# Spacing and offsets of the weight places in a hybrid encoder layer: 1,056 columns apart instead of 1,024, one small offset for four kinds of products

## The chip, the core and the metric

The kernel runs on one core of a Trainium2 chip. The metric is the device time of one execution in microseconds (us); of several runs the median is given. The engines are named as in the profile: PE (TensorE, matrix products, with PEld for its weight loads), DVE (VectorE), ACT (ScalarE), POOL (GpSimd), SP (SyncE, which here only issues transfers).

## What is computed

One layer of an encoder on 512 tokens of width 1,024, all in float32:

```python
h = modulate(rmsnorm(x, norm_ffn1), sh1, sc1)
x = x + 0.5 * g1 * swiglu(h, w_ffn1_in, w_ffn1_out)         # 1024 -> 2 x 2816 -> 1024
h = modulate(rmsnorm(x, norm_mix), sh2, sc2)
qa, ka, va, qb, kb, vb, ga, gb = split(h @ w_in)
ya = window_gqa_sink(rope(qa), rope(ka), va) @ w_branch_a   # 8 heads on 2, window 128
yb = rmsnorm(diff_attention(rope(qb), rope(kb), vb)) @ w_branch_b   # 4 heads, dense
x = x + g2 * ((sigmoid(ga) * ya + sigmoid(gb) * yb) @ w_out)
h = modulate(rmsnorm(x, norm_ffn2), sh3, sc3)
x = x + 0.5 * g3 * swiglu(h, w_ffn2_in, w_ffn2_out)
```

The nine vectors sh, sc and g come from `silu(c) @ w_mod + b_mod`.

## The kernel before

**Three products for one.** Every float32 operand is split into a high part (rounded to the type float32r) and a low part (the rest, float32r too). A product of two such operands is three products on the PE: high times high, high times low, low times high (`mm3` at L173 to L176, `two` at L443 to L445, the opening loop at L681, the projections at L1125 to L1127 and L1144 to L1146). What stays in the array is 128 x 128; what is streamed past it, the moving operand, is 256 or 512 columns wide. A 256-wide product is made wherever a token half is worked on by itself, and in the units described next; all others are 512 wide.

**Stages.** Feed-forward 1: an opening with eight outputs (L681), two plain outputs pairs (L174 to L176), then units of a seven-product scheme on 2 x 2 blocks (class `Unit`, products `a11`, `s1`, `a12`, `a22`, `s4`, `s2`, `s3`, each of 24 matmuls 256 wide), between them the output projection in four chunks (class `Out1`; its last chunk is called `final`, and the last four of its eight rows, `LAST_1`, are made by token halves). Then the mixer: gates, projections `project` and `project_pairs` (here the weights are the moving operand and the hidden state the stationary one), the two attentions interleaved, the two branch projections (`branch`, 512 wide for `w_yb`, by halves for `w_ya`), and the mixing product `w_mix` (eight rows, the last two, `LAST`, by halves). Then feed-forward 2: one plain pair of outputs (class `Plain`), the unit `lead` and then units of the same scheme to the end.

**The places of weights.** A weight tile of 128 x 1,024 columns is loaded into a buffer `raw` (or `u`), and ACT and DVE write its high and low part (`split_from`, L190) into a place. The places lie in two long tiles, `high` and `low`, five places in each (`HILO`), taken in turn by `high_low`; a place that a unit still holds is passed over. Place i begins at column i x 1,024 plus an offset that the caller names, `aside`:

```python
ASIDE = 16
FAR = 64
STEP, STEP_1 = 8, 56
BRANCH_ASIDES = (STEP, ASIDE, ASIDE, ASIDE), (ASIDE, ASIDE, 0, 0)
MIX_ASIDES = 0, 0, 0, 0, 0, 0, ASIDE, ASIDE
```

The units use 16 columns, the opening, the projections, the gates (but one) and the 512-wide rows of `w_mix` use none, `Out1` uses 64 for its 512-wide rows (its tiles have at most 768 columns) and 56 or 16 for its last four rows, and `project_pairs` 16. A full tile of 1,024 columns that is set aside by 16 reaches 16 columns into the next place. A column is 4 bytes.

**The order of the work.** The PE's order is written out by hand (`run_items`, `boundary`, and the list of timed pieces in `Line`); loads are asked for a fixed number of items ahead (`ASK`, `MAKE`). Writing a place waits for the last matmul that read the columns it overlaps.

**Memory.** A core has 229,376 bytes in each partition. Tiles are laid out in the order of their first use, each rounded up to 32 bytes; tiles of one tag share its buffers. The hidden states and the other split operands are in `b8` (8,192 bytes each) and `u4` (4,096 bytes). The last byte used is 229,120.

Of the kernel before, what the change touches and what calls it, by code (L numbers as in the profile page):

```python
# [18 lines left out]
P = 128  # L19
# [79 lines left out]

ASIDE = 16  # L100

FAR = 64


STEP, STEP_1 = 8, 56
BRANCH_ASIDES = (STEP, ASIDE, ASIDE, ASIDE), (ASIDE, ASIDE, 0, 0)
MIX_ASIDES = 0, 0, 0, 0, 0, 0, ASIDE, ASIDE

# [26 lines left out]
def layer(ctx: ExitStack, tc: tile.TileContext, a: dict):  # L135
# [61 lines left out]
    def high_low(n=1024, aside=0, holder=None):  # L197
        while turn[0] % HILO in holders:
            turn[0] += 1
        i = turn[0] % HILO  # L200
        turn[0] += 1
        if holder:
            holders[i] = holder
        i = i * 1024 + aside
        return tuple(t[:, i : i + n] for t in parts)
# [20 lines left out]
    S.activation(small(8), half, AF.Silu)  # L226
    ones = keep([P, P], "ones")
    V.memset(ones, 1.0)
    ident = keep([P, P], "ident")
    make_identity(nc, ident)  # L230

    par = keep([P, NPAR], "par")
    x = [xt() for _ in range(NC)]
    parts, modv = [], []
    for nm, n in (("high", 6), ("low", 9)):
        parts.append(keep([P, HILO * 1024 + ASIDE], nm, F32R))
        modv += [keep([P, NC], f"mod{v}") for v in range(len(modv), n)]
    sub8, lam_s, nlam = (keep([P, n], nm) for nm, n in (("sub8", 1), ("lam_s", 2), ("nlam", 1)))

# [44 lines left out]
    class Norm:  # L284
# [41 lines left out]
        def sums(self, sq, r, first, last):  # L326
            if first:
                self.st[r.start] = bank("op" if r.start else "tp")
            for t in range(r.start // P, r.stop // P):
                i = 2 * (t - r.start // P)  # L330
                PE.matmul(
                    self.st[r.start][:, i : i + 2], sq[:, t * P : (t + 1) * P], ones[:, 0:2],
                    start=first and i == 0, stop=last and (t + 1) * P == r.stop, skip_group_check=True,
                )
# [112 lines left out]
    class Unit:  # L447
# [14 lines left out]

        in_order = ()
        spare, roomy, apart, more = ("s1",), (), (), {"s1": ("s2", "a11"), "s2": ("s4", "a12"), "a11": ("s3", "a21")}
# [16 lines left out]
        def prepare(self, q):  # L481

            if q in self.ready:
                return
            self.ask(q)
            n = self.depth * 2 * P
            if q in self.apart:
                both = b8().rearrange("p a b -> p (a b)")
                hi, lo = both[:, 0:n], both[:, 1024 : 1024 + n]
            else:  # L490
                hi, lo = high_low(n, ASIDE, (self, q))
            t = self.at[q]
# [110 lines left out]
    hh, hl = new_h()  # L603
    ccol = keep([P, 3 * NC], "ccol")[:, 0:NC]
    nc.scalar.dma_start(ccol, a["c"])
# [4 lines left out]
    with tc.manual_schedule(engines=BOUND | {mybir.EngineType.SP, mybir.EngineType.Pool}):  # L610
# [16 lines left out]
        warm(3)  # L627
        w1, pos = {}, []

        def first_loads(k):  # L630
            scale = mod_load(SC1, k)
            if k == 0:
                pos.append(keep([P, NT], "pos", I32))
# [140 lines left out]
    row = u4(F32).rearrange("p a b -> p (a b)")[:, 0:NROW]  # L774
    pos = pos[0]
    freq = keep([P, HD // 2], "freq")
# [56 lines left out]
    class Out1:  # L833
# [13 lines left out]

        def by_halves(self, m):
            return self.final and m >= NC - LAST_1

        def prepare(self, m):
            if m not in self.ready:
                self.ask(m)
                aside = FAR if not self.by_halves(m) else STEP_1 if m == NC - LAST_1 else ASIDE
                if self.final and m == 0:
                    while turn[0] % HILO != 1:
                        turn[0] += 1
                t = self.ready[m] = high_low(self.depth * P, aside, (self, m))
                with tc.issue_after(copied[0]):
                    split_from(*t, self.at[m])  # L860
# [52 lines left out]
    with tc.manual_schedule(engines={mybir.EngineType.SP, mybir.EngineType.Pool}):  # L913
# [4 lines left out]
        for q in range(4, 2 * PLAIN):  # L918

            w, sums_from = loaded1, split[1]  # L920
            if q < 5:
                with tc.issue_after(split[0]), tc.issue_after(split[1]):
                    loaded1 = [load_split(a["w1i"][1, k], aside=ASIDE) for k in range(2)]
            behind = split[1]
# [60 lines left out]
    NF = HD // 2  # L985
    posf = keep([P, NT], "posf")
    V.tensor_copy(posf, pos)
# [70 lines left out]

    def load_main(src, aside=0):

        raw = sbuf("raw", [P, 1024], F32, RAW)
        nc.sync.dma_start(raw, src)
        hi, lo = high_low(aside=aside)
# [67 lines left out]
    def project_pairs(srcs, then):  # L1131
# [3 lines left out]
        for u, src in enumerate(srcs):  # L1135
            wh, wl = load_main(src, ASIDE)
            for t in range(NT):
# [22 lines left out]
    def gates(more=lambda: True):  # L1160
        while gate_next[0] < 16 and more():
            j = gate_next[0]
            gate_next[0] += 1

            wh, wl = load_main(a["w_gate"][j], ASIDE * (j == EARLY_A))
            out = bank("acc")
            for k in range(NC):
                o = k * P
                mm3(out, wh[:, o : o + P], wl[:, o : o + P], hh[k], hl[k], k == 0, k == NC - 1)
                yield MM3  # L1170
            gate_end(j, out)
# [73 lines left out]
    rqb = keep([P, NT, 8], "rqb")  # L1245
    nrqb = keep([P, NT, 8], "nrqb")
    ob_h, ob_l = b8(), b8()
# [145 lines left out]
    def tables_a():  # L1393
# [3 lines left out]
        ka = sbuf("ka", [P, 2, T], F32R, 1)  # L1397
        wa.update(k=(ka[:, 0, :], ka[:, 1, :]), rq=keep([P, NT, 8], "rqa"))

# [197 lines left out]

    def branch(w, j0, o_h, o_l, then, load, r=FULL[0], asides=(0, 0, 0, 0)):
        for u in range(4):
            with tc.issue_after(banded_last[0]):  # L1600
                wh, wl = load(w[u], aside=asides[u])
            for i in range(2):
# [10 lines left out]
    def main():  # L1613
# [31 lines left out]
        for i, r in enumerate(HALVES):  # L1645
            line.drain(lambda: done["a"] >= 2 * i + 2)
            yield from branch(a["w_ya"], 0, *wa["o"], then_b, load_split, r, BRANCH_ASIDES[i])

# [13 lines left out]
    for m in range(NC):  # L1662
        w = load_split(a["w_mix"][m], aside=MIX_ASIDES[m])

# [369 lines left out]
```

## Time and profile before

| | |
|---|---|
| three runs | 1045.71, 1048.36, 1048.68 us; median 1048.36 |
| the profiled execution | 1044.11 us, of which the span from first to last instruction is 1042.3 us |
| granted PE clock in it | 0.999 |
| busy: PE, DVE, ACT, POOL | 99%, 75%, 55%, 16% of the span |
| matmuls | 7,348, and as many weight loads |
| moved by DMA | 220.92 MB |

In the profile a matmul's end is modelled and consecutive matmuls overlap, so its duration (276 ns for most 256-wide ones) is not what it costs. What it costs is the distance from its start to the start of the next one, which is read from the starts in the timeline. The timeline's times begin at the start of the span.

### The profile page before, as it was taken

Reading aid. Unit: us, or ns where it says so; the run is one execution under the profiler, and the core shown is the slowest. Engines: PE = TensorE matmul, PEld = TensorE weight load, DVE = VectorE, ACT = ScalarE, POOL = GpSimd, SP = SyncE. Lnnn points to the kernel's source line nnn. Section 1 sums busy time; section 2 is a strip of 40 time slices with the busy share of each in tenths; the row PEclk is TensorE's granted clock in tenths of the full one; section 3 lists DMA queues with packets and bytes.
Section 4 is the critical chain, followed back from the end, with each engine's and each line's share of the span. In section 5 each row is a group of like instructions: output and inputs, shape, how many; then the busy total and the mean of one; then the engine's idle time right before and its main releaser. Section 6 shows DMA issues by size and latency. Waiting matters only on the chain.

```text
span 1042.3 us, 18751 instructions
## 1 busy us (share of the span) xinstructions
PE 1034.8 (99%) x7348; PEld 953.2 (91%) x7348; DVE 785.5 (75%) x1436; ACT 575.6 (55%) x948; POOL 165.7 (16%) x190
## 2 busy tenths in 40 slices
PE   9999999999999999999999999999999999999998
PEld 6889899899998998899888888989999999999998
DVE  6886667567796679859772588976899777877867
ACT  6664335234454442667785855525867556655553
POOL 1101110110110100543333101001111111112110
PEclk9999999999999999999999999999999999999999
DMA  9977786966984459796646834974498998989874
GB/s 366 346 218 187 242 235 198 275 173 180 259 207 150 149 203 410 232 261 140 179 97 184 242 124 158 366 229 112 98 238 190 244 226 206 231 216 220 208 150 127
DMA packets 68793, 220.92 MB, mean 212 GB/s; under 512 B 8288, under 2 KB 10976, under 8 KB 68704
## 3 DMA queue, kind: packets, MB, share of 16 engines
q1 hardware_dynamic: 46224, 146.52, 38.7%
q0 software_dynamic: 19344, 68.70, 35.1%
q10 hardware_dynamic: 3136, 4.51, 1.2%
q8 instruction: 57, 0.93, 0.3%
q14 instruction: 32, 0.26, 0.1%
HBM read 209.46 MB, written 10.23 MB: 211 GB/s over the span
## 4 chain that ended last, share of the span: by engine, by line
PE 93%; DVE 3%; ACT 3%; issue 0%; DMA 0%; POOL 0%; DVEq 0%; ACTq 0%; POOLq 0%
PE acc L443 7%; PE acc L444 7%; PE acc L445 7%; PE sc L443 6%; PE sc L445 6%; PE sc L444 6%; PE sc L174 5%; PE sc L175 5%; PE sc L176 5%; PE acc L174 4%; PE acc L176 4%; PE acc L175 4%; PE acc L1125 2%; PE acc L1126 2%; PE acc L1127 2%; PE tp L1203 1%
## 5 line engine op out<-in xcount | busy, mean ns | idle before, releaser
L190 ACT CAST high<-raw 128x1024 fp32r<-128x1024 f32 (+2 forms) x160 | 155.9, 985 | 149.8 <-PE sc L175 37.7
L190 DVE TENSOR_TENSOR low<-raw,high 128x1024 fp32r<-128x1024 f32 (+2 forms) x160 | 181.3, 1141 | 49.4 <-ACT high L190 48.5
L443 PE MATMUL acc<-b,high 128*128 128x256 f32 x508 | 140.9, 277 | 0.0
L444 PE MATMUL acc<-b,high 128*128 128x256 f32 x508 | 140.7, 277 | 0.1
L445 PE MATMUL acc<-b,low 128*128 128x256 f32 x508 | 140.6, 277 | 0.0
L445 PE MATMUL sc<-b,low 128*128 128x256 f32 x500 | 138.5, 277 | 0.0
L443 PE MATMUL sc<-b,high 128*128 128x256 f32 x500 | 138.5, 277 | 0.0
L444 PE MATMUL sc<-b,high 128*128 128x256 f32 x500 | 138.4, 277 | 0.0
L190 DVE TENSOR_TENSOR low<-u,high 128x1024 fp32r<-128x1024 f32 (+1 forms) x73 | 87.5, 1200 | 21.8 <-ACT high L190 20.3
L190 ACT CAST high<-u 128x1024 fp32r<-128x1024 f32 (+1 forms) x73 | 75.4, 1036 | 49.1 <-PE sc L175 16.2
L174 PE MATMUL sc<-b,high 128*128 128x512 f32 (+1 forms) x272 | 97.5, 359 | 0.0
L175 PE MATMUL sc<-b,high 128*128 128x512 f32 (+1 forms) x272 | 97.3, 358 | 0.0
L176 PE MATMUL sc<-b,low 128*128 128x512 f32 (+1 forms) x272 | 97.1, 357 | 0.0
L444 PEld LDWEIGHTS acc<-b,high 128*128 128x128 f32 x508 | 95.5, 188 | 0.4 <-DVE b L1818 0.3
L443 PEld LDWEIGHTS acc<-b,high 128*128 128x128 f32 x508 | 95.5, 188 | 0.3 <-ACT f L520 0.2
L445 PEld LDWEIGHTS acc<-b,low 128*128 128x128 f32 x508 | 95.4, 188 | 0.0
L443 PEld LDWEIGHTS sc<-b,high 128*128 128x128 f32 x500 | 94.1, 188 | 0.2 <-ACT f L520 0.2
L445 PEld LDWEIGHTS sc<-b,low 128*128 128x128 f32 x500 | 93.9, 188 | 0.1
L444 PEld LDWEIGHTS sc<-b,high 128*128 128x128 f32 x500 | 93.9, 188 | 0.0
L174 PE MATMUL acc<-b,high 128*128 128x512 f32 (+1 forms) x240 | 89.4, 372 | 0.3 <-DVE u L190 0.3
L176 PE MATMUL acc<-b,low 128*128 128x512 f32 (+1 forms) x240 | 87.1, 363 | 0.0
L175 PE MATMUL acc<-b,high 128*128 128x512 f32 (+1 forms) x240 | 86.9, 362 | 0.0
(387 smaller groups left out, 2713.5 us busy)
## 6 DMA issues: line engine op xcount, KB each, us to landing
u<-w_mod SPq DMA_DIRECT2D x40, 512.0 KB, 8.0
b<-w_mod SPq DMA_DIRECT2D x32, 512.0 KB, 5.7
raw<-w2i SPq DMA_DIRECT2D x31, 512.0 KB, 5.3
u<-w2i POOLq DMA_DIRECT2D x31, 512.0 KB, 7.1
u<-w1u POOLq DMA_DIRECT2D x24, 512.0 KB, 7.4
raw<-w1u SPq DMA_DIRECT2D x24, 512.0 KB, 6.7
raw<-w1o SPq DMA_DIRECT2D x24, 384.0 KB, 4.3
raw<-w_gate SPq DMA_DIRECT2D x16, 512.0 KB, 4.2
```

Of the source, the lines that this page charges most:

```text
L174: PE.matmul(out, wh, xh, start=first, stop=False)
L175: PE.matmul(out, wh, xl, start=False, stop=False)
L176: PE.matmul(out, wl, xh, start=False, stop=last)
L190: last = S.copy(hi, src), V.tensor_tensor(lo, src, f(hi), ALU.subtract)
L443: PE.matmul(out, wh[:, s], xh, start=first and j == 0, stop=False, skip_group_check=True)
L444: PE.matmul(out, wh[:, s], xl, start=False, stop=False, skip_group_check=True)
L445: PE.matmul(out, wl[:, s], xh, start=False, stop=last and j == 1, skip_group_check=True)
L1125: PE.matmul(out[t][:, 0:n], hh[k][:, ht], wh[:, o : o + n], start=k == 0, stop=False)
L1126: PE.matmul(out[t][:, 0:n], hh[k][:, ht], wl[:, o : o + n], start=False, stop=False)
L1127: PE.matmul(out[t][:, 0:n], hl[k][:, ht], wh[:, o : o + n], start=False, stop=k == NC - 1)
L1203: PE.transpose(tp[:, j * P : (j + 1) * P], src, ident)
```

## The change

Places are 1,056 columns apart (`PLACE`), so that a tile set aside does not reach into the next one. The offset becomes a yes or no of 8 columns (32 bytes). It is used by four kinds of products: rows 4 and 5 of the `final` chunk of `Out1`, the second tile of the first half of the `w_ya` branch, row 6 of `w_mix`, and `a11` and `a21` of the `Plain` pair of feed-forward 2. All others have none. To make room, `ones` has 2 columns instead of 128, `nrqb` takes the buffer of `freq` and `rqa` that of `Ckb`; small tiles (`pos`, `ccol`, `sub8`, `lam_s`, `nlam`, the `mod` vectors) are created at other points of the program, two of them with padding. The instructions, their number and their order are the same.

```diff
-ASIDE = 16
-FAR = 64
-STEP, STEP_1 = 8, 56
-BRANCH_ASIDES = (STEP, ASIDE, ASIDE, ASIDE), (ASIDE, ASIDE, 0, 0)
-MIX_ASIDES = 0, 0, 0, 0, 0, 0, ASIDE, ASIDE
+PLACE, ASIDE = 1024 + 32, 8
...
-        i = i * 1024 + aside
+        i = i * PLACE + aside * ASIDE
...
-    ones = keep([P, P], "ones")
+    ones = keep([P, 2], "ones")
...
+    sub8, lam_s, nlam = (keep([P, n], nm) for nm, n in (("sub8", 1), ("lam_s", 2), ("nlam", 1)))
+    pos = keep([P, 4 * NT], "pos", I32)[:, 0:NT]
+    parts, modv = [], []
+    def mods(n):
+        modv.extend(keep([P, NC], f"mod{v}") for v in range(len(modv), n))
+    mods(2)
     x = [xt() for _ in range(NC)]
-    parts, modv = [], []
-    for nm, n in (("high", 6), ("low", 9)):
-        parts.append(keep([P, HILO * 1024 + ASIDE], nm, F32R))
-        modv += [keep([P, NC], f"mod{v}") for v in range(len(modv), n)]
-    sub8, lam_s, nlam = (keep([P, n], nm) for nm, n in (("sub8", 1), ("lam_s", 2), ("nlam", 1)))
+    ccol = keep([P, 2 * NC], "ccol")[:, 0:NC]
+    for nm, n in (("high", 5), ("low", 6)):
+        parts.append(keep([P, (HILO - 1) * PLACE + 1024 + ASIDE], nm, F32R))
+        mods(n)
...
-                hi, lo = high_low(n, ASIDE, (self, q))
+                hi, lo = high_low(n, q in self.aside, (self, q))
...
     hh, hl = new_h()
-    ccol = keep([P, 3 * NC], "ccol")[:, 0:NC]
+    mods(9)
...
-                aside = FAR if not self.by_halves(m) else STEP_1 if m == NC - LAST_1 else ASIDE
+                aside = self.final and 0 <= m - (NC - LAST_1) < 2
...
-                    loaded1 = [load_split(a["w1i"][1, k], aside=ASIDE) for k in range(2)]
+                    loaded1 = [load_split(a["w1i"][1, k]) for k in range(2)]
...
-            wh, wl = load_main(src, ASIDE)
+            wh, wl = load_main(src)
...
-            wh, wl = load_main(a["w_gate"][j], ASIDE * (j == EARLY_A))
+            wh, wl = load_main(a["w_gate"][j])
...
-    nrqb = keep([P, NT, 8], "nrqb")
+    nrqb = sbuf("freq", [P, NT, 8], F32, 1)
...
-        wa.update(k=(ka[:, 0, :], ka[:, 1, :]), rq=keep([P, NT, 8], "rqa"))
+        wa.update(k=(ka[:, 0, :], ka[:, 1, :]), rq=sbuf("Ckb", [P, NT, HD], F32, 1)[:, :, 0:8])
...
-            yield from branch(a["w_ya"], 0, *wa["o"], then_b, load_split, r, BRANCH_ASIDES[i])
+            yield from branch(a["w_ya"], 0, *wa["o"], then_b, load_split, r, (1, None)[i])
...
-        w = load_split(a["w_mix"][m], aside=MIX_ASIDES[m])
+        w = load_split(a["w_mix"][m], aside=m == NC - LAST)
...
+    plain.aside = ("a11", "a21")
```

More of the change, by code (lines that the diff above doesn't have):

```diff
@@ L331, in sums @@
                 PE.matmul(
-                    self.st[r.start][:, i : i + 2], sq[:, t * P : (t + 1) * P], ones[:, 0:2],
+                    self.st[r.start][:, i : i + 2], sq[:, t * P : (t + 1) * P], ones,
                     start=first and i == 0, stop=last and (t + 1) * P == r.stop, skip_group_check=True,
@@ L461, in layer @@
         asked, length = ("s1", "a11", "a12", "a22"), 1.0
-        in_order = ()
+        in_order = aside = ()
         spare, roomy, apart, more = ("s1",), (), (), {"s1": ("s2", "a11"), "s2": ("s4", "a12"), "a11": ("s3", "a21")}
@@ L627, in layer @@
         warm(3)
-        w1, pos = {}, []
+        w1, kept = {}, []
         def first_loads(k):
@@ L632, in first_loads @@
             if k == 0:
-                pos.append(keep([P, NT], "pos", I32))
+                kept.append(keep([P, NT], "posf"))
             shift = mod_load(SH1, k) if k == 0 else None
@@ L774, in layer @@
     row = u4(F32).rearrange("p a b -> p (a b)")[:, 0:NROW]
-    pos = pos[0]
     freq = keep([P, HD // 2], "freq")
@@ L846, in ask @@
                 nc.sync.dma_start(t, a["w1o"][m][:, c : c + n])
-        def by_halves(self, m):
-            return self.final and m >= NC - LAST_1
         def prepare(self, m):
@@ L985, in layer @@
     NF = HD // 2
-    posf = keep([P, NT], "posf")
+    posf = kept[0]
     V.tensor_copy(posf, pos)
@@ L1057, in layer, with load_main @@
     hh, hl = new_h()
-    def load_main(src, aside=0):
+    def load_main(src):
         raw = sbuf("raw", [P, 1024], F32, RAW)
         nc.sync.dma_start(raw, src)
-        hi, lo = high_low(aside=aside)
+        hi, lo = high_low()
         S.copy(hi, raw)
@@ L1595, in window_out, with branch @@
             turns["w"] = (b, g * nk + kc + 1)
-    def branch(w, j0, o_h, o_l, then, load, r=FULL[0], asides=(0, 0, 0, 0)):
+    def branch(w, j0, o_h, o_l, then, load, r=FULL[0], aside=None):
         for u in range(4):
             with tc.issue_after(banded_last[0]):
-                wh, wl = load(w[u], aside=asides[u])
+                wh, wl = load(w[u], **({"aside": True} if u == aside else {}))
             for i in range(2):
```

## The prediction

> **What bounds the kernel now.** I read the page first (busy times, then the chain), then the waits of the PE, then the timeline of the PE in stretches.
>
> ```profile
> span 1042.3 us, 18751 instructions
> ...
> PE 1034.8 (99%) x7348; PEld 953.2 (91%) x7348; DVE 785.5 (75%) x1436; ACT 575.6 (55%) x948; POOL 165.7 (16%) x190
> ...
> PE 93%; DVE 3%; ACT 3%; issue 0%; DMA 0%; POOL 0%; DVEq 0%; ACTq 0%; POOLq 0%
> ```
> ```profile
> PE acc L617 <- POOL ident masks.py:199: 1.3, 1, 1.3
> PE acc L681 <- ACT b L669: 0.4, 2, 0.2
> PE op L331 <- ACT f L292: 0.3, 1, 0.3
> PE acc L174 <- DVE u L190: 0.3, 1, 0.3
> ```
>
> The PE is the bound from beginning to end: 93% of the chain that ended last, and in 1042.3 us it waits for other engines 2.3 us by name. A wait removed elsewhere is worth nothing; what can change the time is what one matmul costs. So the third view is the timeline, for starts of the same kind far enough apart to give a cost to a tenth of a nanosecond.
>
> ```profile
> 60.48 0.39 PE L174 MATMUL acc<-b,high 128*128 128x512 f32 x1
> ...
> 71.36 0.40 PE L174 MATMUL acc<-b,high 128*128 128x512 f32 x1
> ...
> 82.56 0.28 PE L443 MATMUL sc<-u,high 128*128 128x256 f32 x1
> ...
> 99.10 0.28 PE L443 MATMUL sc<-b,high 128*128 128x256 f32 x1
> ...
> 109.30 0.28 PE L443 MATMUL op<-b,high 128*128 128x256 f32 x1
> ...
> 142.65 0.28 PE L443 MATMUL acc<-b,high 128*128 128x256 f32 x1
> ...
> 216.83 0.28 PE L443 MATMUL sc<-u,high 128*128 128x256 f32 x1
> ...
> 219.64 0.28 PE L443 MATMUL acc<-b,high 128*128 128x256 f32 x1
> ...
> 366.33 0.28 PE L174 MATMUL acc<-b,u 128*128 128x256 f32 x1
> ...
> 375.58 0.28 PE L174 MATMUL acc<-b,u 128*128 128x256 f32 x1
> ...
> 481.57 0.28 PE L1145 MATMUL acc<-low,b 128*128 128x256 f32 x1
> ...
> 485.93 0.28 PE L1146 MATMUL acc<-high,b 128*128 128x256 f32 x1
> ...
> 665.39 0.28 PE L174 MATMUL acc<-b,high 128*128 128x256 f32 x1
> ...
> 671.15 0.40 PE L174 MATMUL sc<-b,high 128*128 128x512 f32 x1
> ...
> 734.78 0.28 PE L443 MATMUL sc<-b,high 128*128 128x256 f32 x1
> ...
> 746.09 0.28 PE L443 MATMUL tp<-u,b 128*128 128x256 f32 x1
> ```
>
> Each pair of rows is divided by the products that the code issues between them. The first plain pair of outputs (no offset) is 48 products of 512 columns in 10.88 us: 226.7 ns each. The second pair, the same work with its weights 16 columns aside, is 48 in 11.20 us: **233.3 ns**. Nothing else in the two stretches differs that the PE waits for. At 256 columns: 90 products of units in 10.20 us, 113.3 ns; but 96 of the same form, with the same offsets, in 11.31 us, 117.8 ns; 48 of the last `w_ya` tiles, which have no offset, in 5.76 us, 120.0 ns. So where the operands lie in memory sets the cost, by up to 6% of a product, and at 16 columns aside a 256-wide stream has two cadences, 113.3 and 117.8, which last until something disturbs them.
>
> **The change in addresses.** Laid out in order of first use, each tile rounded to 32 bytes, before has `high` at byte 22,848, `low` at 43,584, the first `b8` at 68,672, the first `u4` at 167,072. After: `half` stays at 4,224; the `sm` tiles end at 5,024, `ones` 5,056, `ident` 5,568, `par` 5,984, three small tiles 6,080, `pos` 6,144, two `mod` 6,208, x 22,592, `ccol` 22,656: there `high` begins, 21,024 bytes long; three `mod` lead to `low` at 43,776; `b8` begins at 69,184, `u4` at 167,584, and the last byte is 229,344 of 229,376. Modulo 256: `b8` stays at 64 and `u4` at 160. The weights were at 64 without offset, at 128 with 16 columns, in both tiles and all places. After, place i of `high` is at 128 + 128 i and of `low` at 128 i: always 0 or 128, and the high and low part of one weight in opposite halves. What follows speaks of the distance, weights minus moving operand, modulo 256 bytes. Measured above: distance 0 costs 226.7 ns at 512 columns and 120.0 at 256; distance 64 costs 233.3 and 113.3 or 117.8. With the moving operand in `u4` (distance -32) 24 products take 2.81 us, 117.1 ns; the gates from `u4` weights (distance 96) 78 in 9.25 us, 118.6 ns; the paired projections, whose weights are the moving operand (distance -64), 37 in 4.36 us, 117.8 ns.
>
> **Part by part.**
>
> *512-wide products.* All had distance 0, but those second 48 and one gate; all get distance 64 or -64, mixed two to one within every three products. Their number:
>
> ```profile
> L174 PE MATMUL sc<-b,high 128*128 128x512 f32 x192 | 74.8, 390 | 0.0
> ...
> L174 PE MATMUL acc<-b,high 128*128 128x512 f32 x176 | 71.3, 405 | 0.3 <-DVE u L190 0.3
> ...
> L175 PE MATMUL acc<-b,high 128*128 128x512 f32 x176 | 68.9, 391 | 0.0
> ...
> L174 PE MATMUL acc<-b,high 128*128 128x256 f32 x64 | 18.1, 283 | 0.0
> ...
> L1125 PE MATMUL acc<-high,b 128*128 128x512 f32 x72 | 28.3, 393 | 0.0
> ...
> L1125 PE MATMUL sc<-high,b 128*128 128x512 f32 x24 | 9.4, 390 | 0.0
> ```
> ```profile
> 0.00:1042.00 1042.00, 44.48 (x198) 1.00 0.75 212
> ```
> ```profile
> L681 PE MATMUL acc<-b,low x24: 389/389/396, 17.7 to 58.7; 128*128 128x512 f32 x24
> ...
> L443 PE MATMUL tp<-b,high x94: 276/276/277, 88.1 to 1020.7; 128*128 128x256 f32 x94
> ```
>
> Three lines of 368 are 1,104, less 48 and 24 already at 64; L681 has 198 by its busy time over the span (the second fence), of which 12 are 256 wide: 186; L1125 to L1127 three times 96. Together 1,032 + 186 + 288 = 1,506. At 233.3 instead of 226.7 that is 6.6 ns each, 9.9 us. Some pay already, in the first products after an interruption: the groups of L174 and L175 have means from 390 up where the median of an undisturbed one is 389 (third fence); an estimate of 1.5 us over all lines. Take **+8.4 us**. Bounds: 0, if -64 undoes it, and 9.9; more than 233.3 no row shows. I take the upper end, as the only row near 64 is the measured 233.3, and each triple has at least one product there.
>
> *256-wide products.* The units (4,140) keep distance 64 for one of the two parts and get -64 for the other. The nearest rows are 113.3 and 117.8 for the one, 117.8 for the other. I take them unchanged, since most stand at 113.3 with 64 alone and the mixture has no row; the bound is all of them at 117.8. Of 4,140, 456 read `u4` and some 400 (the 96 above and the like, counted in the timeline) already run at 117.8, so 3,300 x 4.5 ns, +14.8 us. Downward there are the stretches at 117.8 or 120.0: the 256-wide rows of L174 to L176 have a mean of 283 where 276 would be the good cadence: 432 products at some 5 ns, 2.1 us; in the units some 400 x 4.5 ns, 1.8 us; in the projections 288 x 4.5 ns, 1.3 us. That is at most **-5 us**. The four kinds with 8 columns get distance 96 or -32, and what they are followed by is what they could free: after such a distance the units do come out at 113.3 (from 216.83 the `u4` group, then the good cadence), while a unit that follows 512-wide products (from 142.65) starts slow. I take -1.5 us, about a third.
>
> *Overlap of places, and shared buffers.* The columns shared by neighbours made ACT wait for the PE, not the PE for ACT:
>
> ```profile
> ACT high L190 <- PE sc L175: 53.9, 21, 4.5
> ACT high L190 <- PE acc L444: 44.5, 24, 10.0
> ```
> ```profile
> L190 ACT CAST high<-raw 128x1024 fp32r<-128x1024 f32 (+2 forms) x160 | 155.9, 985 | 149.8 <-PE sc L175 37.7
> L190 DVE TENSOR_TENSOR low<-raw,high 128x1024 fp32r<-128x1024 f32 (+2 forms) x160 | 181.3, 1141 | 49.4 <-ACT high L190 48.5
> ```
>
> ACT and DVE stand behind such waits and with them the next split; what hides that is that weights are asked for items ahead: in the PE's waits only 0.3 us, at L174, is for a split. So 0 to -0.3 us; if that cover were gone, a split's 0.985 us on ACT and 1.141 us on DVE would show at each such place, and no row does. `nrqb` and `rqa` must wait for the last reader of `freq` and `Ckb`; writers and readers are both DVE, in its own order, so no wait is added. `ones`, `pos`, `ccol` and the vectors cost the same elsewhere. No instruction or transfer is added, so no queue gets longer.
>
> Sum against the profiled execution, 1044.11 us: +8.4 - 1.5 = +6.9, so 1051.0. The median of the runs shown, 1048.36, stands 4.25 above that execution; the same +6.9 gives **1055.3**, say 1055.
>
> **The rivals.**
>
> *A: placed so, the 512-wide products pay* (above), 1051 to 1059. For it: 48 products in one unbroken cadence of 233.3. Against: both parts had distance 64 there, never one on each side.
>
> *B: the units lock into the slow cadence too.* Distance -64 has shown nothing but 117.8, and no `u4` group is in the way of that within a unit. Partly or wholly: +8.4 and up to 14.8, 1059 to 1071.
>
> *C: opposite halves cure both, and it is faster.* The two distances 128 apart are not alike (117.1 at -32, 118.6 at 96), so one part's stall might be what puts the other in step, as a disturbance by `u4` does. Then 512-wide products stay at 226.7, slow stretches go: -2 to -6, 1042 to 1046, middle 1044.5. It decides when more than about six in seven of the 1,506 stay at 226.7, since each seventh costs 1.4 us. Against: both cadences known at 64 and -64 would have to be avoided at once.
>
> *D: it does not matter where the places lie.* The 16 columns aside may only mark a stretch that was slow for another reason; then only the 0.3 us is at stake, 1045 to 1051. Against: 226.7 turns to 233.3 at the very product at which the offset begins. The Trainium skill, "SBUF — State Buffer", section "SBUF: two separate sides", has it this way: the PE has ports of its own and never waits on anyone, so by that rule the time would stay 1048. The rows of 60.48 to 82.56 speak against using it to this precision.
>
> **How the numbers follow.** A 0.42, B 0.10, C 0.34, D 0.14. A measurement of this kernel tells about 0.3%, 3.1 us, from no change. Faster: C but for its upper edge, 0.33; same: D and that edge, 0.15; slower: A and B, 0.52. The range takes A, D, the nearer half of C and the nearer half of B: 1043 to 1063; left out are the best of C and the worst of B. If only A holds, 1051 to 1059.
>
> **What would show it.** Durations of the undisturbed 512-wide groups: 392 to 398 ns instead of 389 for A, at L681 and L174 to L176 from the opening on, and starts 233 ns apart; 389 for C. Units at 276 ns for A and C, 281 for B. After the final chunk of `Out1`, row 6 of `w_mix` and the `Plain` pair, 276 ns where 281 and 283 stood, if the 8 columns free the cadence. The PE's waits should stay near 2.3 us; if they grew, my account of the overlap would be wrong. The forecast is wrong if the 512-wide products stay at 389.

## The result and the profile after

The changed kernel takes 1051.14 us (median of 15 runs, 1049.09 to 1054.01), the kernel before 1047.68 us in the same comparison (15 runs, 1044.83 to 1049.17): a ratio of 1.0040, with a 95% interval of 1.0030 to 1.0051. It is slower, by 3.5 us in the medians and some 4 by the ratio. The profiled execution took 1050.02 us, 5.9 more than the 1044.11 of before; that one was faster than all fifteen of this comparison.

The page of the changed kernel (the busy times, the chain):

```profile
span 1048.2 us, 18743 instructions
...
PE 1040.2 (99%) x7348; PEld 953.0 (91%) x7348; DVE 785.8 (75%) x1436; ACT 576.4 (55%) x948; POOL 165.9 (16%) x190
...
PE 91%; DVE 3%; ACT 3%; DMA 1%; issue 1%; POOL 0%; ACTq 0%; DVEq 0%; POOLq 0%
```

The same 7,348 products take 5.4 us more of the PE's time, and the span grew by 5.9. The PE is still the bound. Its waits for other engines, the four longest, and ACT's for the places:

```profile
PE acc L617 <- POOL ident masks.py:199: 1.4, 1, 1.4
PE sc L443 <- ACT f L520: 0.6, 1, 0.6
PE acc L681 <- ACT b L669: 0.4, 2, 0.2
PE op L331 <- ACT f L292: 0.3, 1, 0.3
```
```profile
ACT high L183 <- PE sc L168: 54.7, 21, 4.0
ACT high L183 <- PE acc L444: 44.9, 23, 10.1
```

One wait is new (0.6 us, a product sum that ACT had not yet copied out of the bank). What ACT waits for the PE before it can write a place was 53.9 and 44.5 us and is 54.7 and 44.9: that full tiles no longer share columns gained nothing here. The rest is the cost of single products. Groups by shape (lines L174 to L176 of before are L167 to L169 now, L190 is L183), and the starts in the timeline that answer to those shown of before:

```profile
L169 PE MATMUL sc<-b,low 128*128 128x512 f32 x192 | 75.8, 395 | 0.0
L167 PE MATMUL sc<-b,high 128*128 128x512 f32 x192 | 75.6, 394 | 0.0
...
L167 PE MATMUL acc<-b,high 128*128 128x256 f32 x64 | 17.9, 279 | 0.0
```
```profile
61.39 0.39 PE L167 MATMUL acc<-b,high 128*128 128x512 f32 x1
...
72.46 0.39 PE L167 MATMUL acc<-b,high 128*128 128x512 f32 x1
...
83.61 0.28 PE L443 MATMUL sc<-u,high 128*128 128x256 f32 x1
...
86.45 0.28 PE L443 MATMUL sc<-b,high 128*128 128x256 f32 x1
...
92.16 0.28 PE L443 MATMUL sc<-b,high 128*128 128x256 f32 x1
...
94.91 0.28 PE L443 MATMUL acc<-u,high 128*128 128x256 f32 x1
...
100.48 0.28 PE L443 MATMUL sc<-b,high 128*128 128x256 f32 x1
...
110.68 0.28 PE L443 MATMUL op<-b,high 128*128 128x256 f32 x1
...
219.75 0.28 PE L443 MATMUL sc<-u,high 128*128 128x256 f32 x1
...
222.60 0.28 PE L443 MATMUL acc<-b,high 128*128 128x256 f32 x1
...
740.34 0.28 PE L443 MATMUL sc<-b,high 128*128 128x256 f32 x1
...
751.51 0.28 PE L443 MATMUL tp<-u,b 128*128 128x256 f32 x1
```

The first plain pair, 48 products 512 wide, took 10.88 us and takes 11.07: 230.6 ns each instead of 226.7. The second pair, which was at 233.3, is at 232.3 (11.15 us). Units in their good cadence stay where they were: 90 products in 10.20 us, 113.3 ns. The `u4` group is slower: 24 products in 2.85 us, 118.8 ns instead of 117.1. The 96 products at 740.34, which cost 117.8 ns, are at 116.4: partly freed. And one stretch is newly slow, 72 products from 86.45 in 8.46 us, 117.5 ns: its first 48, to 92.16, cost 119.0 each, although one of their two parts lies at 64 and the other at -64.

Summing the start-to-start distances of all products of a kind over the two traces gives the account of the 5.9 us:

| kind of product | number | before, us | after, us | difference, us |
|---|---|---|---|---|
| 512 wide, weights from places | 1,290 | 297.78 | 302.06 | +4.3 |
| 512 wide, places streamed | 288 | 65.71 | 66.72 | +1.0 |
| 256 wide, weights from places | 4,080 | 468.36 | 467.90 | -0.5 (cadence -0.8, interruptions +0.3) |
| 256 wide, the same, `u4` streamed | 456 | 53.50 | 54.71 | +1.2 (cadence +0.6, one wait +0.6) |
| all others | 1,234 | 150.84 | 150.70 | -0.1 |

The 0.8 us in the third line come from the 432 products of rows made by token halves, whose mean without interruptions goes from 117.6 to 115.6 ns. The units alone, 3,636 products with weights from places, do not gain: 113.85 ns before and 113.88 after.

### The profile page after: what moved, and what is told of

Same layout as the page of the kernel before. It is cut to its first block, busy times and chain, and to the rows that moved or that the text cites. A ratio compares the mean times of both kernels' runs of the same rounds, so it can differ in the third digit from the quotient of the medians.

```text
span 1048.2 us, 18743 instructions
## 1 busy us (share of the span) xinstructions
PE 1040.2 (99%) x7348; PEld 953.0 (91%) x7348; DVE 785.8 (75%) x1436; ACT 576.4 (55%) x948; POOL 165.9 (16%) x190
## 4 chain that ended last, share of the span: by engine, by line
PE 91%; DVE 3%; ACT 3%; DMA 1%; issue 1%; POOL 0%; ACTq 0%; DVEq 0%; POOLq 0%
PE acc L444 6%; PE acc L443 6%; PE acc L445 6%; PE sc L445 6%; PE sc L443 6%; PE sc L444 6%; PE sc L167 5%; PE sc L169 5%; PE sc L168 5%; PE acc L167 5%; PE acc L169 5%; PE acc L168 5%; PE acc L1121 2%; PE acc L1123 2%; PE acc L1122 2%; PE tp L1199 2%
## 5 line engine op out<-in xcount | busy, mean ns | idle before, releaser
L183 ACT CAST high<-raw 128x1024 fp32r<-128x1024 f32 (+2 forms) x160 | 155.9, 984 | 150.1 <-PE sc L168 37.9
L183 DVE TENSOR_TENSOR low<-raw,high 128x1024 fp32r<-128x1024 f32 (+2 forms) x160 | 181.3, 1140 | 52.5 <-ACT high L183 48.7
L183 DVE TENSOR_TENSOR low<-u,high 128x1024 fp32r<-128x1024 f32 (+1 forms) x73 | 87.5, 1200 | 21.9 <-ACT high L183 20.6
L183 ACT CAST high<-u 128x1024 fp32r<-128x1024 f32 (+1 forms) x73 | 75.3, 1034 | 51.8 <-PE sc L168 16.8
L167 PE MATMUL sc<-b,high 128*128 128x512 f32 (+1 forms) x272 | 98.3, 361 | 0.0
L169 PE MATMUL sc<-b,low 128*128 128x512 f32 (+1 forms) x272 | 98.2, 361 | 0.0
L167 PE MATMUL acc<-b,high 128*128 128x512 f32 (+1 forms) x240 | 89.6, 373 | 0.2 <-DVE u L183 0.2
L169 PE MATMUL acc<-b,low 128*128 128x512 f32 (+1 forms) x240 | 87.2, 363 | 0.0
```

The source lines that it names most:

```text
L167: PE.matmul(out, wh, xh, start=first, stop=False)
L169: PE.matmul(out, wl, xh, start=False, stop=last)
L183: last = S.copy(hi, src), V.tensor_tensor(lo, src, f(hi), ALU.subtract)
```

## The experiments

The theory after the result: the start-to-start distance of a product is set by the distance of its two operands in memory (the one that stays in the array minus the one that is streamed, modulo 256 bytes). At 512 columns 0 is cheapest; a mixture of 64 and -64 costs about the mean of the two; at 256 columns opposite halves free the units from the slow cadence. Rivals: the period is 128 and not 256 bytes; it is the mixture of halves that costs; the placing does nothing and something else moved.

**One part at distance 0, the other at 128.** The changed kernel, all weights of 512-wide products 16 columns aside:

```diff
-PLACE, ASIDE = 1024 + 32, 8
+PLACE, ASIDE, WIDE = 1024 + 32, 8, 2
...
-    loaded1 = [load_split(a["w1i"][0, k]) for k in range(2)]
+    loaded1 = [load_split(a["w1i"][0, k], aside=WIDE) for k in range(2)]
```

(and so at every place where such weights are loaded; three small tiles became one to make room.)

> The changed kernel, with the weights of every 512-wide product set 16 columns (64 bytes) aside, so that their distance to the moving operand is 0 in one of the two parts and 128 in the other, instead of 64 and -64. If the loss is one of distance and what counts is the distance modulo 128, all 512-wide products come back to 226.7 ns (durations of 389 ns) and the kernel gains the 5.3 us that they lost in the profile: 1045 to 1047 us, a ratio to before of 0.997 to 0.999. If it counts modulo 256, the part at distance 128 does not come back: products between 226.7 and 233.3 ns, 1048 to 1052. If the loss is not one of distance (rival: the spacing of the places itself), nothing changes: 1051.

1051.74 us, ratio 1.0052 (1.0035 to 1.0069): nothing came back.

```profile
60.69 0.39 PE L167 MATMUL acc<-b,high 128*128 128x512 f32 x1
...
82.99 0.28 PE L444 MATMUL sc<-u,high 128*128 128x256 f32 x1
```

96 products in 22.30 us, 232.3 ns, where all-0 gives 226.7. The time alone would fit the second and the third expectation; the single products decide. A distance of 128 bytes is not as good as 0: the period is longer than 128. What 128 costs by itself is not shown, since no kernel has both parts there. The 512-wide products with weights from places cost 5.4 us more than before, more than in the changed kernel.

**Both parts in the same half.** The changed kernel, with the low part taken from the next place, so that both are at 64 or both at -64:

```diff
-        return tuple(t[:, i : i + n] for t in parts)
+        j = (i // PLACE + 1) % HILO * PLACE + i % PLACE
+        return parts[0][:, i : i + n], parts[1][:, j : j + n]
```

> The changed kernel, but the low part of a weight goes to the place after that of its high part (taken cyclically), so that in four places of five both parts have the same distance: 64 in places 0 and 2, -64 in places 1 and 3, and one of each in place 4 as in the change. If 512-wide products cost by distance, places 0 and 2 show 233.3 ns, place 4 the mixture's 231, and places 1 and 3 tell what -64 costs alone: about 229 if the mixture is a mean, 233.3 if the two distances are alike and the mixture is better than either. In time 1050 to 1054. If the place does not matter, all places show 231 and the time is 1051.

1050.89 us, ratio 1.0040 (1.0024 to 1.0056).

```profile
61.38 0.39 PE L167 MATMUL acc<-b,high 128*128 128x512 f32 x1
...
66.89 0.39 PE L167 MATMUL acc<-b,high 128*128 128x512 f32 x1
...
72.45 0.39 PE L167 MATMUL acc<-b,high 128*128 128x512 f32 x1
...
78.04 0.40 PE L167 MATMUL acc<-b,high 128*128 128x512 f32 x1
```

The tile from 61.38 has both parts at -64: 24 products in 5.51 us, 229.6 ns. The tile from 72.45 has both at 64: 24 in 5.59 us, 232.9 ns. Over this trace, interruptions left out, the weights from places cost 229.7 ns where all three products of a triple lie at -64 (452 products) and 232.9 where all lie at 64 (436); where they are mixed, 231.8. So it is not the mixture that costs: each of the two distances has its price, and their mixture lies between.

**Everything at 64.** The kernel before with all weights 16 columns aside, wide or not:

```diff
-        i = i * 1024 + aside
+        i = i * 1024 + ASIDE
```

> The kernel before, with every weight set 16 columns aside in every place: the distance is 64 for both parts of all weights, places are still 1024 columns apart and none overlap. This is the part of the change that moves the 512-wide weights, alone and unmixed. If distance is the cause, the 512-wide products show 392 to 398 ns instead of 389, 233.3 ns from start to start, and the kernel loses the 8.4 us of the prediction: 1055 to 1057. If the loss of the change comes from putting high and low part in opposite halves or from the wider spacing, this kernel stays at 1047 to 1049.

1052.61 us, ratio 1.0057 (1.0037 to 1.0076).

```profile
61.85 0.40 PE L172 MATMUL acc<-b,high 128*128 128x512 f32 x1
...
84.25 0.28 PE L441 MATMUL sc<-u,high 128*128 128x256 f32 x1
```

96 products in 22.40 us, 233.3 ns; the same is the mean over the 1,255 such products of the trace that nothing interrupts. Weights from places at 512 columns cost 6.6 us more, streamed places (whose distance is then -64) 0.6 us: 7.2 us where 8.4 were expected, and a median below the 1055 to 1057 expected. This kernel keeps the spacing of before, so the loss is the placing alone.

**Without the 8 columns.** The changed kernel, its one small offset left out:

```diff
-        i = i * PLACE + aside * ASIDE
+        i = i * PLACE
```

> The changed kernel without the 8 columns of the four kinds: all weights at their places. If the 8 columns free the 256-wide products that follow them from the slow cadence, the stretches after them (second half of the last rows of the output projection, the second w_ya half, the first unit of feed-forward 2) go back to 118 ns from 113.3, and about 1 us is lost: 1052. If the mixture of distances alone frees them, the time is that of the changed kernel, or better by up to 0.5 us, as the set-aside groups themselves run at 118 to 119 ns: 1050.5 to 1051.5.

1049.67 us, ratio 1.0028 (1.0015 to 1.0040): not the loss of the first case expected. Whether it is better than the changed kernel stays open: the intervals overlap, and in the traces the 4,080 products take 468.0 us against 467.9, 1.4 less in cadence and 1.4 more in 15 further interruptions. What the 8 columns do shows in the stretches:

```profile
742.14 0.28 PE L443 MATMUL sc<-b,high 128*128 128x256 f32 x1
...
753.04 0.28 PE L443 MATMUL tp<-u,b 128*128 128x256 f32 x1
```

The 96 products at 117.8 ns before and 116.4 in the changed kernel are at 113.5 here (10.90 us). The products set aside by 8 columns cost 118 to 119 ns in the changed kernel, and free nothing that the opposite halves had not freed.

**Opposite halves for the units alone, first try.** If each distance has its price, the kernel before can keep distance 0 for 512-wide products and give only the 256-wide ones 64 and -64.

```diff
-        i = i * 1024 + aside
-        return tuple(t[:, i : i + n] for t in parts)
+        i = i * 1024
+        each = aside if isinstance(aside, tuple) else (aside, aside)
+        return tuple(t[:, i + s : i + s + n] for t, s in zip(parts, each))
...
-                hi, lo = high_low(n, ASIDE, (self, q))
+                hi, lo = high_low(n, OPPOSITE_U4 if q == "s1" and self.operand.__name__ != "act_operand" else OPPOSITE, (self, q))
...
-            wh, wl = load_main(src, ASIDE)
+            wh, wl = load_main(src, PAIRS)
```

with `PAIRS, OPPOSITE, OPPOSITE_U4 = 48, (16, 48), (40, 8)`; to keep the distances, `ones` was cut to 2 columns and four `mod` vectors moved from behind `high` to behind `low`.

> The kernel before, whose 512-wide products stay at distance 0 (weights minus moving operand, modulo 256 bytes). Only 256-wide products are moved: in the units the high part goes to distance 64 and the low part to -64 (offsets of 16 and 48 columns; of 40 and 8 for the weights that meet an operand in u4), and the streamed places of the paired projections go from -64 to 64. Theory (the cost is that of the distance, kind by kind, and opposite halves free the units from the slow cadence): 512-wide products as before, 227.6 ns; units 113.6 to 113.9 instead of 114.1, so -0.8 to -1.9 us on 4,080; products with u4 streamed 113.8 instead of 116.9, -1.4 us on 456; paired projections 114.8 instead of 117.8, -0.9 us on 288. Sum -3 to -4 us, a ratio of 0.996 to 0.997. Rival (the u4 products at 117 are what puts the units in step; without them a slow stretch lasts until the next 512-wide product): the units rise towards 117.8 in many stretches, up to +10 us, a ratio above 1.000. Second rival (distance is not what matters, but which neighbours share columns): no change on u4 and the paired projections, and ACT's waits for the longer overlap cost up to 1 us.

The second kernel has `OPPOSITE, OPPOSITE_U4 = (16, 16), (40, 40)`:

> The same kernel, but both parts of the units' weights at distance 64 (16 columns as before; 40 and 40 where the operand is in u4), so that only the u4 products and the paired projections differ from the kernel before. Theory: u4 products -1.4 us, paired projections -0.9 us, the units' slow stretches after 512-wide products stay (114.1 ns) : -2.3 us, a ratio of 0.998, and 1 to 2 us above the kernel with opposite halves. Rival (the u4 products disturb the slow cadence away): without that disturbance the units' slow stretches grow longer than in the kernel before, 115 to 117 ns, +4 to +12 us.

1063.65 us, ratio 1.0159 (1.0133 to 1.0184), and 1054.02 us, 1.0068 (1.0046 to 1.0089). Both were a mistake in the design. Places are 1,024 columns apart here, and tiles with different offsets follow each other: one set aside by 40 or 48 shares columns with a neighbour set aside by 8 or 16 while both are still to be read, and these columns hold what was written last. So part of the units' weights is not the right one, and tiles that should have been independent wait for each other. Waits of the PE in the first of the two:

```profile
PE sc L177 <- DVE low L191: 2.0, 1, 2.0
PE acc L445 <- ACT f L522: 1.9, 2, 1.5
PE sc L445 <- ACT high L191: 1.9, 2, 1.1
PE acc L177 <- DMA low<-w_gate: 1.4, 1, 1.4
```

In all, interruptions cost 14.1 us more in this kernel's 4,080 products with weights from places. The prices of the single products came out near what was expected all the same: units at 64 with -64 113.7 ns, `u4` streamed at 64 or -64 114.0 (48 of the 456 products stayed where they were), paired projections 115.2, 512-wide 227.8. In the second kernel the units, both parts at 64, have 114.0: not the 115 to 117 of its rival.

**Uniform offsets.** Three kernels in which no tile overwrites columns of another that are still to be read. First only `u4` is moved, by a longer tile ahead of it:

```diff
-    ccol = keep([P, 3 * NC], "ccol")[:, 0:NC]
+    ccol = keep([P, 8 * NC], "ccol")[:, 0:NC]
```

> The kernel before with one small tile (ccol) 160 bytes longer, so that all u4 buffers lie 160 bytes later and their distance to the places' 16 columns is 64 instead of -32; the places and everything ahead of u4 stay. Theory (the distance alone sets the pitch): the 456 products that stream u4 go from 116.9 to 113.8 ns, -1.4 us; the 144 whose weights are in u4 go from distance 96 to 0, 118.7 to 120.0, +0.2 us; sum -1.2 us, a ratio of 0.999. Rival (the u4 products at 117 put the units in step): their pitch falls all the same, but the units' stretches at 117.8 get longer, from 114.1 to 115 ns and more on 4,080 products, +4 us or worse. Second rival (the tile u4 itself costs, not its address): no change.

1059.98 us, ratio 1.0125 (1.0107 to 1.0142). One tile 160 bytes longer makes the kernel 14 us slower, and the first rival names the reason.

```profile
99.79 0.28 PE L443 MATMUL sc<-b,high 128*128 128x256 f32 x1
...
110.39 0.28 PE L443 MATMUL op<-b,high 128*128 128x256 f32 x1
...
218.90 0.28 PE L443 MATMUL sc<-u,high 128*128 128x256 f32 x1
...
221.73 0.28 PE L443 MATMUL acc<-b,high 128*128 128x256 f32 x1
```

The 90 products that cost 113.3 ns before cost 117.8 (10.60 us), at the same addresses. The `u4` group does not get cheaper either: 24 in 2.83 us, 117.9. Over the trace 3,900 products with `b8` streamed and both parts at 64 (the units and the rows of the same offset) have a mean of 117.4, where before they had 114.1, and `u4` 117.8. With both parts at 64 the units have two cadences, and the `u4` group as it lay before was what put them into the good one.

The distance of -32 is not needed for that. In the second kernel of the first try this `u4` group is at 64 like the units around it, and nothing interrupts these 192 products:

```profile
217.82 0.28 PE L445 MATMUL acc<-b,high 128*128 128x256 f32 x1
...
220.65 0.29 PE L445 MATMUL sc<-u,high 128*128 128x256 f32 x1
...
223.39 0.28 PE L445 MATMUL acc<-b,high 128*128 128x256 f32 x1
...
239.74 0.28 PE L445 MATMUL acc<-u,high 128*128 128x256 f32 x1
```

The first 24 cost 117.9 ns, the 24 of `u4` 114.2, the 144 behind them 113.5: freed, at a distance of 64 throughout. The two kernels differ in where `u4` lies: 96 bytes from `b8` modulo 256 there, as in the kernel before, and 0 here. So a distance by itself does not decide the cadence; a step in the addresses from one group to the next fits both kernels, though no run changes that step alone. What stands ahead can also leave it good: in the kernel before, the units behind 512-wide products at distance 0 start at 117.8 (from 142.65), but with everything at 64 they start in the good cadence.

```profile
145.28 0.28 PE L441 MATMUL acc<-b,high 128*128 128x256 f32 x1
...
148.00 0.28 PE L441 MATMUL sc<-u,high 128*128 128x256 f32 x1
```

These are 24 in 2.72 us, 113.3 ns.

Then the paired projections too, units as before, and last the units in opposite halves (16 and 48 columns in all units, in rows 6 and 7 of `w_mix` and, both parts at 48, in one gate):

```diff
+PAIRS, UNITS = 48, (16, 48)
...
-                hi, lo = high_low(n, ASIDE, (self, q))
+                hi, lo = high_low(n, UNITS, (self, q))
...
-        w = load_split(a["w_mix"][m], aside=MIX_ASIDES[m])
+        w = load_split(a["w_mix"][m], aside=UNITS if m >= NC - LAST else 0)
```

(this is the second kernel; in the first `UNITS` is `(16, 16)`, and the `w_mix` line is as before. Both have the shorter `ones` and the moved `mod` vectors of the first try.)

> As the run before, and the streamed places of the paired projections at 48 columns (distance 64 instead of -64); both parts of the units' weights at distance 64 as in the kernel before. Offsets are the same in all units, so no place of a unit reaches into another unit's columns. Theory: u4 -1.2 us, paired projections -0.75 us (2.6 ns on 288), sum -2.0 us, a ratio of 0.998. Rival (longer overlap of neighbours, 48 columns in place of 16, holds up the splits as in the two runs with mixed offsets): some us slower around the projections.

> As the run before, and the low part of the units' weights, of rows 6 and 7 of w_mix and of one gate at 48 columns, the high part at 16: distance 64 and -64. Theory (opposite halves free the units from the slow cadence): units at 113.75 instead of 114.1, -1.4 us, so -3.4 us in all, a ratio of 0.9967, the fastest of these kernels. Rival (opposite halves do nothing for 256-wide products; it was what went before them that freed them in the changed kernel): the same as the run before, 0.998. Second rival (48 columns of overlap in the low tile cost waits of DVE): 1 us or more above the run before.

1063.03 us, ratio 1.0160 (1.0146 to 1.0174), against 1044.51 us, ratio 0.9976 (0.9964 to 0.9988). `u4` lies where `b8` does modulo 256 in both, and nothing in it frees the units: in the first they stay at 117.5 ns on average, far from the 0.998 expected, in the second they have 113.5.

```profile
101.66 0.28 PE L444 MATMUL sc<-b,high 128*128 128x256 f32 x1
...
111.86 0.28 PE L444 MATMUL op<-b,high 128*128 128x256 f32 x1
...
220.05 0.28 PE L444 MATMUL sc<-u,high 128*128 128x256 f32 x1
...
222.77 0.28 PE L444 MATMUL acc<-b,high 128*128 128x256 f32 x1
```

In the second: 90 products in 10.20 us, 113.3; 24 of `u4` in 2.72 us, 113.3. Both kernels together show that opposite halves do it here: 18.5 us lie between them, and of the 16.9 us between the two profiled spans 14.9 lie in the 256-wide products with weights from places. New interruptions cost the second kernel 3.7 us of these products' time against before; by its ratio it gains 2.5 us where 3.4 were expected. In both, `b8` and the places lie 32 bytes further on modulo 256 than before, at the same distances, and the 512-wide products still cost 227.8 ns: as far as 32 bytes tell, it is the distance that sets their price, not the address.

Opposite halves are no full cure. In the changed kernel, whose `u4` lies 96 bytes from `b8`, units in opposite halves run at 119 behind some `u4` groups: the 48 products from 86.45, and 24 each from 283.63, 784.59 and 880.53. The means of some stretches, from the starts in the traces (ns, distances over 130 ns, which are interruptions, left out; `u4` at 64 is the first of these three kernels, opposite halves the last):

| stretch (start in before) | products | before | after | after, no 8 columns | `u4` at 64 | opposite halves |
|---|---|---|---|---|---|---|
| unit behind 512-wide products, 142.7 | 24 | 117.8 | 113.5 | 113.5 | 117.8 | 114.2 |
| `u4` group, 216.8 | 24 | 117.0 | 118.8 | 118.8 | 117.8 | 113.3 |
| unit behind it, 219.6 | 144 | 113.4 | 113.3 | 113.3 | 117.8 | 113.3 |
| last rows of `Out1`, 340.5 | 84 | 117.5 | 116.8 | 113.4 | 117.5 | 117.5 |
| behind `w_mix`, 721.7 | 36 | 117.8 | 118.1 | 113.6 | 113.7 | 114.3 |
| behind that, 734.8 | 96 | 117.8 | 116.5 | 113.5 | 117.8 | 113.5 |

**The rest of the 256-wide products.** First the last rows of `Out1` and all `w_ya` tiles, then the rows of `Out1` alone (without the first two lines of this diff):

```diff
-BRANCH_ASIDES = (STEP, ASIDE, ASIDE, ASIDE), (ASIDE, ASIDE, 0, 0)
+BRANCH_ASIDES = (UNITS,) * 4, (UNITS,) * 4
...
-                aside = FAR if not self.by_halves(m) else STEP_1 if m == NC - LAST_1 else ASIDE
+                aside = FAR if not self.by_halves(m) else UNITS
```

> As the kernel with opposite halves and uniform offsets (0.9976), and the remaining 256-wide products with weights from places follow: the last four rows of Out1 and all w_ya tiles by halves get 16 and 48 columns too, so that no 256-wide product is left at distances -32, 0, 32 or 64 for both parts. Theory (the offsets of 8, 56 and 0 columns free nothing; any distance but 64 with -64 only costs): the 102 products at 116.8 to 120.0 and the 221 at 115.5 come down to 113.5, -0.9 us; a ratio of 0.996 to 0.997. Rival (those offsets are needed as the step that frees what follows, as u4 was in the kernel before): the stretches after them stay or rise to 117.8, no gain, 0.998. Second rival (48 columns of overlap with the w_mix rows that follow at offset 0): waits of the PE for a split there, 1 us or more lost.

1048.16 us, ratio 1.0012 (0.9997 to 1.0028). The products came down to 113.5 ns, and one wait took more than that back:

```profile
PE sc L174 <- ACT high L190: 3.0, 1, 3.0
```

The stretch from the last `w_ya` tiles into `w_mix` is 4.25 us longer. By the layout, a `w_ya` tile that reaches 16 columns (high part) or 48 (low part) into the next place keeps the `w_mix` row there, at offset 0, from being written; the trace does not name the tile, and the next run tests it.

> As the run before, but the w_ya tiles keep their offsets of the kernel before (8, 16 and 0 columns), so that only the last four rows of Out1 differ from the kernel at 0.9976. Theory (the loss of the run before was the one wait at the w_mix rows behind the w_ya tiles): that wait of 3.0 us is gone; the stretch after Out1's last rows, 144 products at 117.5 to 117.8, comes to 113.5, -0.6 us; a ratio of 0.996 to 0.9975. Rival (Out1's rows caused part of it): a ratio of 0.999 or more, with the wait still there.

1042.18 us, ratio 0.9960 (0.9943 to 0.9977): the wait is gone, and this is the lowest ratio of all the kernels, though its interval overlaps that of the 0.9976.

```profile
span 1041.1 us, 18751 instructions
```
```profile
0.00:20.00 20.00, 18.65 (x78) 0.84 0.93 353
```

Its span is 1.2 us below that of before although its first 20 us (second fence: window, length, PE busy, granted clock, DMA share, GB/s) ran at a granted clock of 0.84, where before had 1.00, and its opening products (L682, L681 of before) start 2.15 us later (17.93 against 15.78). By the sums over the trace, `u4` gives 1.5 us, the paired projections 0.7, the units 1.1 net of 1.7 for new interruptions.

## Why the prediction was right, and where it was not

*The forecast case.* A held: placed so, the 512-wide products pay, and the kernel is slower. The durations of the 512-wide groups rose from 389 to 392 to 396, as it said they would, their starts came to 231 ns apart and not 233, and the PE's waits stayed small (2.9 us against 2.3). That the two profiles differ by 5.9 us, near the +6.9 of the sum, is in part luck: its two terms were wrong in opposite directions, by 3.1 and 2.2 us.

*The term of the 512-wide products*, +8.4 us, measured +5.3. The mechanism and the number of products were right; the price was too high. I took 233.3 ns for all, "as the only row near 64 is the measured 233.3". The products that lie at -64, about half of them, cost 229 to 230 where nothing else is mixed in, so the mean is 231, and 1,578 products at some 3.4 ns come to 5.3 us. The row was of one distance, and the sum used it for two.

*The term of the 256-wide products*, -1.5 us, measured +0.7 with its waits. The units gained nothing (113.85 and 113.88 ns): what they won behind 512-wide products they lost behind `u4` groups. The 0.8 us of cadence came from the rows by token halves, and 0.3 went to an interruption. What the sum left out is the `u4` group: I counted its 456 products among those that would not change, but their distance became -32 for one part and 96 for the other, and the cadence went from 117.0 to 118.3 on average, +0.6 us; the wait of 0.6 us stands at one of them as well.

*The 8 columns.* The step "what they are followed by is what they could free" failed. What frees these stretches in the changed kernel is the opposite halves; without the 8 columns the stretches behind `w_mix` and in `Out1` are better still (113.4 to 113.6 instead of 116.5 to 118.1). The idea behind it was not wrong: in the kernel before the `u4` group does work as such a step, and taking it away costs 14 us. But the reason given, that a group at 96 or -32 frees, does not hold, since a `u4` group at 64 freed the units too; and no such step was needed where the parts lie in opposite halves and `u4` lies with `b8`.

*Overlap and shared buffers*, 0 to -0.3 us: ACT's waits for the PE did not move when the shared columns went, so these were not what made it wait, as the prediction had read it. Overlap costs where offsets differ: 14 us in many waits, and by the layout the single one of 3.0 us.

*From the profile to the median.* The sum was +6.9, the profiles differ by 5.9, the medians by 3.5. The step used the three runs shown, whose median was 1048.36; fifteen runs gave 1047.68. The profiled execution of before stands 3.6 us under that median and the one of the changed kernel only 1.1 under its own, so their difference is 2.5 us too large for the median. About a microsecond of it is two interruptions, and no run here shows in how many executions they occur.

*The rivals.* B, units locked into the slow cadence, happened only in short stretches (48 and three times 24 products at 119); but the lock is real, and the two kernels with both parts of the units at 64 and `u4` where `b8` lies modulo 256 show it, at +14 to +17 us. C was wrong for the 512-wide products: it needed one rule for both widths, and 226.7 belongs to distance 0 alone. For the units it was right in the kernels of the end, and in the changed kernel only behind 512-wide products. D is refuted by the kernel with everything at 64, which changes nothing but the placing and loses 6.6 us in the 512-wide products. The Trainium skill, "SBUF — State Buffer", section "SBUF: two separate sides", says that the PE never waits on anyone; read as covering the placing of its own operands, that would have left this kernel at the time of before. The trace differs from that by 6.6 ns in 226.7.

*Still open.* Why the distance sets the price: the runs give the price of each distance, not the part of the chip where it arises. Nor is it shown whether a step in the addresses, and of which operand, is what changes the cadence of a 256-wide stream, or why opposite halves mostly keep it out of the slow one.

## What to carry to other kernels

Where the PE is busy all the time, the addresses of its two operands are part of the cost: take the start-to-start distance of one product from the timeline, sort it by the distance of weights and moving operand, and price each distance by itself before one is given to two kinds of product. A cadence that is good may hang on what was streamed just before, even on a neighbour that looks slow, so try a move of one buffer alone before counting its gain. And offsets that differ between tiles sharing columns make waits: a place must be as far from the next as its largest offset, or all offsets in a run the same.

## What the runs showed of the hardware that was not expected

- A 128x512 float32r product costs 226.7 ns start to start at a distance of 0 modulo 256 bytes, 229 to 230 at -64, 233 at 64; with one part at 0 and the other at 128 the mean is 232.3.
- A 128x256 product has at distance 64 two cadences, 113.3 and 117.8 ns, each of which lasts for hundreds of products; 120.0 at distance 0. With its two parts at 64 and -64 the units have 113.5 on average in the kernel that places `u4` with `b8`; in the changed kernel up to 48 such products in a row stand at 119.
- Which of the two cadences holds depends on what was streamed before: with `u4` 96 bytes from `b8` modulo 256 the products at 64 had a mean of 114.1, with `u4` at 0 from it 117.4, their own addresses being the same. Behind 512-wide products at distance 0 they start at 117.8, behind such at 64 at 113.3.
- The distance counts too where the weights are the streamed operand: the paired projections, 256 wide, cost 117.8 ns at -64 and 115 at 64.
